# A hybrid decoder block: the input projection as a stage of its own, with its feature-major part in seven half products, and mixers beside another block's output products

## The chip, the cores and the metric

The kernel runs on one core of a Trainium2 chip. The core has a matrix engine (TensorE, PE in the profile; its weight loads are PEld), three engines for element-wise work (VectorE or DVE, ScalarE or ACT, GpSimd or POOL) and a queue for transfers (SyncE or SP). Matrix products write to PSUM, everything else lies in SBUF or in DRAM. The metric is the device time of one execution in microseconds, the median of several runs.

## What is computed

A sequence of 2048 rows of 1024 values passes one decoder block, in float32. The first half is two mixers side by side over one input projection; the second half is a gated feed-forward part, which the change leaves alone.

```python
mod = c @ w_ada + b_ada                      # shift, scale, gate for both halves
h = modulate(rms_norm(x, g_pre_mix), shift_m, scale_m)
proj = h @ w_in                              # 1024 -> 4872 columns
q_a, k_a, v_a, q_m, k_m, v_m, o_m, i_m, f_m, g_a, g_m = jnp.split(proj, ...)
y_a = sliding_window_attention(rope(q_a), rope(k_a), v_a, sinks)      # window 128
q_m, k_m = split(silu(causal_depthwise_conv([q_m, k_m])))             # 4 taps
y_m = sigmoid(o_m) * head_layer_norm(mlstm_chunkwise(q_m, k_m, v_m, i_m, f_m))
merged = sigmoid(g_a) * (y_a @ w_branch_attn) + sigmoid(g_m) * (y_m @ w_branch_mlstm)
x = x + gate_m * rms_norm(merged @ w_out, g_post_mix)
h2 = modulate(rms_norm(x, g_pre_ffn), shift_f, scale_f)
x = x + gate_f * rms_norm((silu(h2 @ w_ffn_gate) * (h2 @ w_ffn_up)) @ w_ffn_down, g_post_ffn)
```

## The kernel before

Each operand of a large product is split into a rounded part and a rest (`hi`, `lo`, type float32r), and a product is three matrix instructions, hi x hi, hi x lo and lo x hi (`mm3`, L273), each of 128 rows of weights and 512 columns. The weights come by DMA in pieces of about 1 MB (`raw`), ScalarE makes `hi` (L259, L256, L1120) and VectorE `lo` (L260, L257, L1121).

The first half goes block by block (`block`, L656), four blocks of 512 rows. In a block come, in this order: q, k and v of the attention and v of the mLSTM with tokens on the partitions ("token-major", `token_group`, L308: 96, 96 and 96 instructions, those of k, v and the gates 264 columns wide); gate A, the mLSTM's q and k, and its output gate with features on the partitions ("feature-major", `feature_tiles`, L302); branch A (`branch_tiles`, L1016); gate B, feature-major again; branch B; and `w_out` with the norm and the residual (`residual_out`, L518). Feature-major are 28 tiles of 128 columns, each 8 slices of k times three instructions. They read the transposed, normed and modulated rows `hhi` and `hlo`, which `hprep` (L477) makes for the next block while `residual_out` runs.

The mixers are written as generators: `q_stream`, `k_stream`, `gates`, `attention` (L797), `chunk_state` (L916), `chunk_out` (L951). `spawn` puts one on a list, and `tick` (L223), called behind every three matrix instructions, takes the next step of each generator that is due by a clock `now`, which adds up estimated instruction times; the number that a generator yields is its distance to the next step (L38 to L43). `finish` (L230) takes all steps that are left at once. So attention is spread over the products of v, gate A and so on, the mLSTM over the branch and gate B products, and the modulation's weights (`ada_stream`, L448) over everything. The order written so is a priority; the framework's scheduler then fixes each engine's order of instructions and may let one that is ready go ahead.

Buffers: nine of 8 KB per partition (`big`), six of 2 KB (`tx`), nine of 2 KB (`tm`), two for raw weights, four for splits; four PSUM banks for products (`acc`) and four for all else (`mix`). Gates, convolution outputs and branch results of a block stay in `big` buffers from their product to their use.

The feed-forward part works on 1024 rows at once and already uses seven half products for eight (the Winograd form of Strassen's scheme): both operands are cut in two along k and along rows or columns, `PROD` (L1098) lists the seven pairs, `a_operands` (L1259) makes the weight sums on VectorE, `h_combine` (L1198) the sums of h, and `combine` (L1319) adds the products to the four quarters of the result. It has its own loop `run2` (L1130), which runs behind that of the first half (`run`, L342).

## Time and profile before

| what | value |
|---|---|
| median of 3 runs | 2773.7 us (2771.84 to 2776.06) |
| the profiled execution, its time | 2771.54 us |
| its span, first to last instruction | 2769.8 us |
| ScalarE busy | 1233.1 us, 45% |
| GpSimd busy | 153.1 us, 6% |
| DMA | 402.63 MB, 145 GB/s over the span |
| transfers of `w_in` | 76 of 1024 KB, 5.1 us to landing |
| mean granted clock of TensorE | 0.994 |

In the rows of the profile a line begins with the line of the program, the engine and the operation; then come output and inputs by the program's names, the shapes, and the count. Behind the bar stand the busy time in us, the mean duration of one in ns, and the idle time of that engine just before these instructions with what ended it. The rows by stretch give, for each engine, busy us and the number of instructions, then TensorE's granted clock, the share of the DMA engines and the GB/s. Records of matrix instructions overlap, since they are pipelined.

### The profile page before, as it was taken

Reading aid. Unit: us, or ns where it says so; the run is one execution under the profiler, and the core shown is the slowest. Engines: PE = TensorE matmul, PEld = TensorE weight load, DVE = VectorE, ACT = ScalarE, POOL = GpSimd, SP = SyncE. Lnnn points to the kernel's source line nnn. Section 1 sums busy time; section 2 is a strip of 40 time slices with the busy share of each in tenths; the row PEclk is TensorE's granted clock in tenths of the full one; section 3 lists DMA queues with packets and bytes.
Section 4 is the critical chain, followed back from the end, with each engine's and each line's share of the span. In section 5 each row is a group of like instructions: output and inputs, shape, how many; then the busy total and the mean of one; then the engine's idle time right before and its main releaser. Section 6 shows DMA issues by size and latency. Waiting matters only on the chain.

```text
span 2769.8 us, 35110 instructions
## 1 busy us (share of the span) xinstructions
PE 2704.9 (98%) x12654; PEld 2199.7 (79%) x12654; DVE 1922.7 (69%) x3802; ACT 1233.1 (45%) x2285; POOL 153.1 (6%) x201
## 2 busy tenths in 40 slices
PE   6999999999999999999999999999999999999998
PEld 4778878788877888768887888887777888888886
DVE  7768657587674876657776777776676767666456
ACT  4543365433554335544363343334554333333444
POOL 2100001001010010110100000000000000000000
PEclk9999999999999999999999999999999999999999
DMA  7233353242552424523356555545666333233566
GB/s 236 88 111 103 100 180 123 80 137 80 169 163 65 135 86 139 180 67 97 98 168 216 172 176 181 175 152 194 203 236 210 130 102 108 98 111 131 189 212 213
DMA packets 280533, 402.63 MB, mean 145 GB/s; under 512 B 19220, under 2 KB 176536, under 8 KB 280360
## 3 DMA queue, kind: packets, MB, share of 16 engines
q1 hardware_dynamic: 280360, 400.40, 44.3%
q8 instruction: 99, 1.62, 0.2%
q14 instruction: 74, 0.61, 0.1%
HBM read 320.62 MB, written 79.73 MB: 145 GB/s over the span
## 4 chain that ended last, share of the span: by engine, by line
PE 87%; DVE 5%; DMA 4%; ACT 2%; issue 1%; POOL 0%; SPq 0%; DVEq 0%; POOLq 0%; ACTq 0%
PE acc L204 63%; PE mix L204 22%; PE mix L209 2%; DVE hl L1121 1%; DMA raw<-in_w_ffn_down_dram 1%; DVE tm L424 1%; DMA tx<-in_w_ada_dram 0%; ACT hl L1120 0%; DMA raw<-in_w_ffn_gate_dram 0%; DMA raw<-in_w_in_dram 0%; DMA raw<-as_d 0%; DMA x1n<-tx 0%; ACT big L1222 0%; POOL rs L472 0%; DMA w<-x 0%
## 5 line engine op out<-in xcount | busy, mean ns | idle before, releaser
L1120 ACT CAST hl<-raw 128x512 fp32r<-128x512 f32 x564 | 337.1, 620 | 400.2 <-PE mix L204 173.3
L1121 DVE TENSOR_TENSOR hl<-raw,hl 128x512 fp32r<-128x512 f32 x564 | 377.1, 687 | 169.5 <-ACT hl L1120 167.0
L259 ACT CAST whi<-raw 128x1024 fp32r<-128x1024 f32 (+1 forms) x208 | 212.1, 1020 | 501.0 <-PE acc L204 439.1
L260 DVE TENSOR_TENSOR wlo<-raw,whi 128x1024 fp32r<-128x1024 f32 (+1 forms) x208 | 247.4, 1189 | 181.0 <-ACT whi L259 178.2
L204 PE MATMUL acc<-hhi,wlo 128*128 128x512 f32 x896 | 353.9, 395 | 0.0
L204 PE MATMUL acc<-hhi,whi 128*128 128x512 f32 x896 | 352.4, 393 | 0.0
L204 PE MATMUL acc<-hlo,whi 128*128 128x512 f32 x896 | 351.8, 393 | 0.0
L204 PE MATMUL acc<-big,hl 128*128 128x512 f32 x1056 | 254.0, 389 | 0.6 <-ACT w L1328 0.6
L204 PE MATMUL acc<-hl,hl 128*128 128x512 f32 x1008 | 237.0, 393 | 6.9 <-DVE hl L1121 4.3
L204 PEld LDWEIGHTS acc<-big,hl 128*128 128x128 f32 x1056 | 198.0, 188 | 42.3 <-ACT w L1328 1.1
L204 PEld LDWEIGHTS acc<-hl,hl 128*128 128x128 f32 x1008 | 187.1, 188 | 52.6 <-DVE hl L1121 9.5
L204 PEld LDWEIGHTS acc<-hhi,wlo 128*128 128x128 f32 x896 | 168.3, 188 | 42.4 <-issue 8.1
L204 PE MATMUL mix<-big,hl 128*128 128x512 f32 x704 | 197.6, 392 | 3.2 <-DVE big L1257 3.2
L204 PEld LDWEIGHTS acc<-hlo,whi 128*128 128x128 f32 x896 | 168.3, 188 | 37.8 <-issue 3.2
L204 PEld LDWEIGHTS acc<-hhi,whi 128*128 128x128 f32 x896 | 168.4, 188 | 37.2 <-issue 4.1
L204 PE MATMUL mix<-hl,hl 128*128 128x512 f32 x792 | 182.4, 390 | 2.0 <-ACT hl L1120 1.3
L204 PEld LDWEIGHTS mix<-hl,hl 128*128 128x128 f32 x792 | 148.0, 188 | 35.5 <-DVE hl L1121 2.7
L204 PE MATMUL acc<-whi,big 128*128 128x512 f32 x512 | 166.0, 396 | 0.0
L204 PE MATMUL acc<-big,whi 128*128 128x512 f32 x512 | 158.4, 394 | 0.0
L204 PEld LDWEIGHTS mix<-big,hl 128*128 128x128 f32 x704 | 132.9, 189 | 32.0 <-DVE big L1257 4.4
L204 PE MATMUL acc<-whi,hhi 128*128 128x512 f32 (+1 forms) x384 | 133.3, 373 | 22.1 <-DVE tx L530 8.9
L204 PE MATMUL acc<-wlo,hhi 128*128 128x512 f32 (+1 forms) x384 | 140.7, 370 | 2.6 <-DVE wlo L260 2.6
(335 smaller groups left out, 4746.6 us busy)
## 6 DMA issues: line engine op xcount, KB each, us to landing
raw<-in_w_in_dram SPq DMA_DIRECT2D x76, 1024.0 KB, 5.1
as_d<-w SPq DMA_DIRECT2D x154, 256.0 KB, 2.2
raw<-as_d SPq DMA_DIRECT2D x70, 512.0 KB, 3.5
raw<-in_w_ffn_gate_dram SPq DMA_DIRECT2D x22, 1024.0 KB, 5.3
raw<-in_w_ffn_up_dram SPq DMA_DIRECT2D x22, 1024.0 KB, 6.3
raw<-ws_d SPq DMA_DIRECT2D x40, 512.0 KB, 4.3
tx<-in_w_ada_dram SPq DMA_DIRECT2D x64, 256.0 KB, 3.1
raw<-in_w_out_dram SPq DMA_DIRECT2D x16, 1024.0 KB, 5.1
```

The costliest lines, as they stand in the source:

```text
L204: T.matmul(o, lhsT=lhsT, rhs=rhs, start=start, stop=stop, skip_group_check=resumed)
L209: T.transpose(o, i, ident[:k, :k])
L259: A.copy(hv, src)
L260: V.tensor_tensor(lv, src, hv.bitcast(F32), op=ALU.subtract)
L424: V.scalar_tensor_tensor(acc, raw[:, k, :], c_, acc, op0=ALU.mult, op1=ALU.add)
L1120: A.copy(v(hi), src)
L1121: V.tensor_tensor(v(lo), src, v(hi).bitcast(F32), op=ALU.subtract)
```

## The change

The input projection becomes a stage in front of the mixers. It goes over two halves of 1024 rows (`feature_major(j)`), and its feature-major columns (28 tiles) are made by `pair_parts`, the seven products of the feed-forward part, two column tiles and two blocks of 512 rows at a time. The sums of h that this needs come from a new generator `ha_stream`; the normed rows of the third and the fourth block go through DRAM (`norm_stream`, `xn_d`). The quarter of h that the half products don't use as it is (first half of the features, second block of the pair) goes to DRAM for the token-major products (`h12_d`), and so does the last quarter of the second pair until its buffer is free (`h22_d`). The token-major columns are made with eight full products as before, block by block (`token_major(b)`), ahead of, between and behind the two feature-major stages. All results of the projection are written to DRAM: `q_d`, `kv_d`, `vm_d`, and `fm_d` for the two gates (the sigmoid is taken first), the convolved q and k, and the output gate. In the convolution the first tap goes to ScalarE; the scale of the output gate goes there too.

The mixers of a block are one generator, `mixers(b)`, which loads what it needs from DRAM: first rotary tables, then k, the gates, q, the attention, and then the mLSTM. `mixers(0)` is spawned in front of `token_major(3)`, and `mixers(b + 1)` at the start of `merge(b)`. `merge(b)` holds the branch products of block b, A and B now by turns, and `w_out` with the residual; its gates are loaded from `fm_d` into `tx` buffers. The generators' distances are as before. The gains of the residual (`gg_m`) and the pools of the mixers are opened behind `token_major(2)`, in the memory of the projection stage. `run2` goes; one loop `run` takes both halves.

The core of the diff:

```diff
...
+    def row_norms(xb):
+
+        ss = small.tile([P, 4], F32, tag="ss", name=nm("ss"), bufs=4)
+        for t in range(2):
+            for hf in range(2):
+                junk = tx([P, 512])
+                A.activation(junk, xb[:, t, hf * 512:(hf + 1) * 512], AF.Square, accum_out=ss[:, 2 * hf + t:2 * hf + t + 1])
+        V.tensor_tensor(ss[:, 0:2], ss[:, 0:2], ss[:, 2:4], op=ALU.add)
+        r = rsqrt_of_sumsq(ss[:, 0:2], 2)
+        for t in range(2):
+            A.activation(xb[:, t, :], xb[:, t, :], AF.Copy, scale=r[:, t:t + 1])
+
...
+    q_d = [tc.dram_tile([TB, 512], F32, name=f"q_d{b}") for b in range(NBLK)]
+    kv_d = [tc.dram_tile([TB, 264], F32, name=f"kv_d{b}") for b in range(NBLK)]
+    vm_d = [tc.dram_tile([TB, 512], F32, name=f"vm_d{b}") for b in range(NBLK)]
+    fm_d = {n: [tc.dram_tile([P, w, TB], F32, name=f"{n}_d{b}") for b in range(NBLK)]
+            for n, w in (("ga", 8), ("gm", 8), ("qk", 8), ("om", 4))}
+    xn_d = {b: tc.dram_tile([TB, D], F32, name=f"xn_d{b}") for b in range(2, NBLK)}
+    h12_d = [tc.dram_tile([P, 2, 4, TB], F32, name=f"h12_d{j}") for j in range(NB2)]
+    h22_d = tc.dram_tile([P, 2, 4, TB], F32, name="h22_d")
+
+    hhi = hpool.tile([P, KD, TB], F32R, tag="hhi", name="hhi")
+    hlo = hpool.tile([P, KD, TB], F32R, tag="hlo", name="hlo")
+    hat = [hap.tile([P, 4, TB], F32R, name=f"ha{x}") for x in ("T2h", "T2l", "T4h")]
+    hap.tile([P, 8], F32, name="hap_end")
+    HA = {"11": [hhi[:, :4, :], hlo[:, :4, :]], "21": [hhi[:, 4:, :], hlo[:, 4:, :]], "T2": hat[:2], "T4": [hat[2], None],
+          "T1": [None, None], "T3": [None, None], "22": [None, None]}
+
...
+        for k in range(4):
+            v = {}
+            for i in range(1 - j if j < 2 else 0, 2):
+                for half in range(2):
+                    kk = k + 4 * half
+                    if j:
+                        xk = unit().rearrange("p (t c) -> p t c", t=NT)
+                        nc.sync.dma_start(xk, xn_d[2 * j + i][:, kk * P:(kk + 1) * P].rearrange("(t p) c -> p t c", p=P))
+                    v[half, i] = xk if j else None
+            if j:
+                yield 3000.0
+            for half, i in v:
+                kk = k + 4 * half
+                ps = mix_tile()
+                for t in range(NT):
+                    transpose(ps[:, t * P:(t + 1) * P], v[half, i][:, t, :] if j else xb[t // 2][:, t % 2, kk * P:(kk + 1) * P])
+                q = unit()
+                A.activation(q, ps, AF.Identity, scale=s1[:, kk:kk + 1], bias=sh1[:, kk:kk + 1])
+                v[half, i] = q
+                yield 1200.0
+
+            def halves(name):
+                return ha_part(name, 0)[:, k, :], ha_part(name, 1)[:, k, :]
+
+            def known(name):
+                return [p_.bitcast(F32) for p_ in halves(name)]
+
+            t1 = unit()
+            if j:
+                for half, name in ((0, "11"), (1, "21")):
+                    split_unit(v[half, 0], *halves(name))
+                    yield 1200.0
+                V.tensor_tensor(t1, v[0, 1], v[0, 0], op=ALU.subtract)
+            else:
+                h_, l_ = known("11")
+                V.tensor_tensor(t1, v[0, 1], h_, op=ALU.subtract)
+                V.tensor_tensor(t1, t1, l_, op=ALU.subtract)
+            t2 = unit()
+            V.tensor_tensor(t2, v[1, 1], t1, op=ALU.subtract)
+            split_unit(t2, *halves("T2"))
+            yield 1200.0
+            t4 = unit()
+            if j:
+                V.tensor_tensor(t4, v[1, 0], t2, op=ALU.subtract)
+            else:
+                h_, l_ = known("21")
+                V.tensor_tensor(t4, h_, t2, op=ALU.subtract)
+                V.tensor_tensor(t4, t4, l_, op=ALU.add)
+            split_unit(t4, *halves("T4"))
+            yield 1200.0
+            split_unit(t1, *halves("T1"))
+            yield 1200.0
+            V.tensor_tensor(t2, v[1, 1], v[0, 1], op=ALU.subtract)
+            split_unit(t2, *halves("T3"))
+            yield 1200.0
+            for name, d_, half in (("22", h22_d if j else None, 1), ("12", h12_d[j], 0)):
+                if d_ is None:
+                    split_unit(v[half, 1], *halves(name))
+                else:
+                    hl = [au([P, TB], F32R) for _ in range(2)]
+                    split_unit(v[half, 1], *hl)
+                    for i in range(2):
+                        nc.sync.dma_start(d_[:, i, k, :], hl[i].bitcast(F32))
+                yield 1200.0
+
...
+    def token_major(b, lhs):
+
+        def stash(dst, n):
+            def evac(t, ps):
+                u = unit()
+                A.copy(u[:, :n], ps[:, :n])
+                nc.sync.dma_start(dst[t * P:(t + 1) * P, :], u[:, :n])
+            return evac
+
...
+    def lhs_second(kk, t):
+        return tuple(p_[:, kk % 4, t * P:(t + 1) * P] for p_ in (F["h12"] if kk < 4 else HA["22"]))
+
+    def load_h12(j):
+        F["h12"] = [big([4, TB], F32R) for _ in range(2)]
+        for i in range(2):
+            nc.sync.dma_start(F["h12"][i].bitcast(F32), h12_d[j][:, i])
+
...
+        for kind, p in (("ga", 0), ("ga", 1), ("qk", 0), ("ga", 2), ("ga", 3), ("qk", 1), ("gm", 0), ("gm", 1), ("qk", 2),
+                        ("gm", 2), ("qk", 3), ("gm", 3), ("om", 0), ("om", 1)):
+            c0 = {"ga": C_GA, "gm": C_GM, "qk": C_QM, "om": C_OM}[kind] + p * 256
...
+                def taps():
+                    V.tensor_copy(u[:, 0:3], hist[:, i, :])
+                    V.tensor_copy(hist[:, i, :], u[:, TB:TB + 3])
+                    ac = st["ac"] = unit()
+                    A.activation(ac, u[:, 0:TB], AF.Identity, scale=col("conv_w", i), bias=col("conv_b", i))
+                    for q in range(1, 4):
+                        V.scalar_tensor_tensor(ac, u[:, q:q + TB], col("conv_w", q * 8 + i), ac, op0=ALU.mult, op1=ALU.add)
+
+                def silu():
+                    sg = unit()
+                    A.activation(sg, st["ac"], AF.Sigmoid)
+                    V.scalar_tensor_tensor(sg, st["ac"], 1.0 if i < 4 else MD ** -0.5, sg, op0=ALU.mult, op1=ALU.mult)
+                    put("qk", b, i, sg)
+
+                later.extend([taps, silu])
...
+            for part in pair_parts(raw_cols(w_in, KD, c0, 256), HA, new, done):
+                part.weave = True
+                part.after = a_step
+                yield part
+
...
+        p0.close()
+        F["mpool"] = p1.enter_context(tc.tile_pool(name="mpool", bufs=1, reuse_waits="tile"))
+        MX["gg"] = F["mpool"].tile([P, D], F32, name="gg_m")
+        F["tpool"] = p1.enter_context(tc.tile_pool(name="tpool", bufs=1, reuse_waits="tile"))
+        kvp = MX["kvp"] = p1k.enter_context(tc.tile_pool(name="kvp", bufs=1, side="right", reuse_waits="tile"))
...
+        def q_all(t):
+            raw = tm([P, HQ * HD])
+            nc.sync.dma_start(raw, q_d[b][t * P:(t + 1) * P, :])
+            yield 3000.0
+            yield from q_stream(t, rope(raw, HQ, t))
...
+        yield from wait([spawn(k_stream(t), 1000.0 * t) for t in range(NT)])
+        gs = spawn(gates(), 2000.0)
+        for t in range(NT):
+            nc.sync.dma_start(vmt[:, t, :, :MD], vm_d[b][t * P:(t + 1) * P, :].rearrange("p (h d) -> p h d", h=MH))
+        yield from wait([spawn(q_all(t), 3000.0 * t) for t in range(NT)])
+        att = [spawn(attention_pair((0, 2)), L_QK), spawn(attention_pair((1, 3)), L_QK + L_ATT2)]
+        for n, kind, i0 in (("km", "qk", 4), ("qm", "qk", 0), ("om", "om", 0)):
+            nc.sync.dma_start(big_of(n), fm_d[kind][b][:, i0:i0 + 4, :])
+        yield from wait(att + [gs])
+        yield from mlstm()
+        yield from wait(R["outs"])
...
+        def begin():
+            finish([R["mx"]])
+            if not last:
+                RB[b + 1]["mx"] = spawn(mixers(b + 1), 500.0)
+                R["mh"], R["ml"] = ([t[:, :4, :], t[:, 4:, :]] for t in
+                                    (hpool.tile([P, KD, TB], F32R, tag=g, name=nm(g)) for g in ("hhi", "hlo")))
+            else:
+                finish(R_ada)
+                R["mh"], R["ml"] = ([big([4, TB], F32R) for _ in range(2)] for _ in range(2))
+                open_hc()
+
+        yield begin
...
+                        gs_ = [tx([P, TB]) for _ in range(2)]
+                        for j in range(2):
+                            nc.sync.dma_start(gs_[j], fm_d[gate][b][:, i + j, :])
...
+        for i, (pa, pm) in enumerate(zip(branch(w_ba, True, ("yah", "yal"), "ga", evac_a), branch(w_bm, False, ("ymh", "yml"), "gm", evac_m))):
+            if last and i == 2:
+                yield lambda: R.update(hc=spawn(h_combine(0, *HC_FROM_MIXER), 3000.0))
+            yield pa
+            yield pm
+        yield from residual_out(KD, lambda kk, t: tuple(R[m][kk // 4][:, kk % 4, t * P:(t + 1) * P] for m in ("mh", "ml")),
+                                a["w_out"][0], big, load_rows(x_d[b * TB:(b + 1) * TB, :], last), MX, x1[b],
+                                None if last else x1n[b], tm if last else tx)
...
+    def program():
+        for ch in ADA:
+            yield lambda ch=ch: first_h(*ch)
+        yield lambda: F.update(ha=spawn(ha_stream(0), 2000.0))
+        yield from token_major(0, lhs_first)
+        yield lambda: finish([F["ha"]])
+
+        def beside_first():
+            F["nx"] = spawn(norm_stream(), 4000.0)
+            R_ada.append(spawn(ada_stream([(2, "gate"), (4, "scale"), (3, "shift"), (5, "gate")], 3300.0), 20000.0))
+
+        yield beside_first
+        for j in range(NB2):
+            yield from feature_major(j)
+            yield lambda j=j: load_h12(j)
+            if j == 0:
+                def next_ha():
+                    finish([F["nx"]])
+                    F["ha"] = spawn(ha_stream(1), 0.0)
+
+                yield next_ha
+                yield from token_major(1, lhs_second)
+                yield lambda: finish([F["ha"]])
+                yield rest_of_ha
+        yield flush_later
+        yield from token_major(2, lhs_first)
+        yield lambda: finish(R_ada)
+        yield open_mixers
+        yield lambda: RB[0].update(mx=spawn(mixers(0), 500.0))
+        yield from token_major(3, lhs_second)
+        for b in range(NBLK):
+            yield from merge(b)
+        yield open_ffn
         yield rest_of_hc
         yield load_gg
         for b2 in range(NB2):
             yield from gate_up(b2)
             yield from down(b2)
 
...
```

457 lines of the change are left out of this document (193 added, 264 removed).

## The prediction

> **What bounds the kernel now.** I read the page first, then the stretches of 50 us one after another, then the waits of TensorE, then the order of time of single engines where the change cuts in.
>
> ```profile
> span 2769.8 us, 35110 instructions
> PE 2704.9 (98%) x12654; PEld 2199.7 (79%) x12654; DVE 1922.7 (69%) x3802; ACT 1233.1 (45%) x2285; POOL 153.1 (6%) x201
> PE 87%; DVE 5%; DMA 4%; ACT 2%; issue 1%; POOL 0%; SPq 0%; DVEq 0%; POOLq 0%; ACTq 0%
> L204 PE MATMUL acc<-hhi,wlo 128*128 128x512 f32 x896 | 353.9, 395 | 0.0
> ```
>
> TensorE is busy 98% of the span and carries 87% of the chain that ended last. The busy time of a group can't be used as its price, since a product is recorded with 395 ns while others overlap it. The price is the spacing: products in a stretch that holds nothing else.
>
> ```profile
> core 0: us, PE busy (x) PEld busy (x) DVE busy (x) ACT busy (x) POOL busy (x), PEclk, DMA share, GB/s
> 400.00:450.00 50.00, 46.01 (x262) 39.31 (x261) 33.58 (x98) 28.23 (x60) 4.89 (x9) 0.97 0.66 212
> 750.00:800.00 50.00, 44.99 (x249) 38.45 (x248) 36.14 (x106) 29.92 (x64) 6.02 (x12) 1.00 0.76 248
> 900.00:950.00 50.00, 50.00 (x222) 41.41 (x221) 39.49 (x69) 18.38 (x27) 0.00 (x0) 1.00 0.46 132
> 1100.00:1150.00 50.00, 46.74 (x250) 39.98 (x248) 32.69 (x81) 26.18 (x54) 4.52 (x8) 0.97 0.72 240
> 1450.00:1500.00 50.00, 44.24 (x179) 34.81 (x178) 35.23 (x62) 18.76 (x35) 3.19 (x4) 0.93 0.66 237
> 2200.00:2250.00 50.00, 50.00 (x222) 41.42 (x221) 33.41 (x54) 17.57 (x31) 0.00 (x0) 1.00 0.27 90
> ```
>
> Both the feature-major stretch (900 to 950) and the FFN stretch, which already uses seven products for eight (2200 to 2250), hold 222 products in 50 us: **0.2252 us each**, clock 1.00. So a product of 512 columns costs the same in either scheme. TensorE loses time only at the seams between blocks: 4.0, 5.0 and 3.3 us idle where a block begins (400, 750, 1100) and 5.8 us where the FFN begins (1450). The granted clock of 0.97, 0.97 and 0.93 in three of these stretches costs 1.5, 1.5 and 3.5 us more. That makes 24.6 us. The largest of the waits behind it:
>
> ```profile
> PE acc L204 <- DVE tx L530: 8.9, 6, 2.3
> PE acc L204 <- ACT w L1322: 2.0, 1, 2.0
> ```
>
> **The change, part by part.** *Products removed.* Groups hhi,wlo, hhi,whi and hlo,whi are the feature-major part: 28 tiles of 128 columns, 8 slices of k, 4 blocks, 896 in each of three groups, 2688 together. Seven for eight leaves 2352. 336 fewer at 0.2252 us are **75.7 us**, all on the engine that sets the end. Transposes stay 128 in number for h.
>
> *Work added beside those products.* One pair of column tiles for 1024 rows is 84 products, 18.9 us. VectorE gets for it 7 splits, 4 sums of weights and 4 sums of products, each an operation of 128x512.
>
> ```profile
> L1121 DVE TENSOR_TENSOR hl<-raw,hl 128x512 fp32r<-128x512 f32 x564 | 377.1, 687 | 169.5 <-ACT hl L1120 167.0
> L1257 DVE TENSOR_TENSOR big<-w,big 128x512 fp32r<-128x512 f32 x8 | 5.2, 686 | 7.0 <-DMA w<-hc_d 7.0
> 1487.86 2.49 DVE L1257 TENSOR_TENSOR big<-w,big 128x512 fp32r<-128x512 f32 x4
> L899 DVE SCALAR_TENSOR_TENSOR tx<-tx,cols,tx 128x512 f32<-128x512 f32 x96 | 72.0, 750 | 2.7
> L424 DVE SCALAR_TENSOR_TENSOR acc_ada<-tx,c_sb,acc_ada 128x256 f32<-128x256 f32 x112 | 56.6, 506 | 7.7 <-DMA tx<-in_w_ada_dram 6.5
> ```
>
> Four such operations in a row took 2.49 us: (2.49 - 0.686) / 3 = 0.60 us from start to start, though each is recorded with 0.686. So a pair costs VectorE 15 x 0.60 = 9.0 us of 18.9, 126 us over 14 pairs (265 us). The convolution for 1024 rows adds three of the L899 kind and one more sum per tile, 16 tiles, 16 x (3 x 0.67 + 0.60 + 0.2) = 45 us, and the modulation (L424, 112 of them, nearly all beside the first of the two stages) up to 47 us: at most 218 of 265 us, hidden. ScalarE has less than half of its time taken in the like FFN stretch (17.6 of 50 us) and gains a few operations of 0.6 us per pair. Stalls here: 0 to 10 us by bursts; I take 2.
>
> *Operands of the half products.* ha_stream makes T1 to T4 of h: 12 operations of VectorE per k, 4 k, 48 x 0.60 = 29 us, once beside token_major(0) and once beside token_major(1), each of 192 products of 512 and 96 of 264 columns: 192 x 0.2252 + 96 x 0.116 (by columns) = 54.3 us. VectorE has 11 us of weight splits of its own there, so it fits; but the stream starts behind an x load, and the first products need its results at once. Cover gone, it would be up to 10 us at each; the load of h12 (2 MB) in front of token_major(1) another 10 us at the 212 GB/s of the 400 to 450 stretch. Behind that first product of token_major(1) the 191 others of its group stand in TensorE's order, and their evacuation. Bounds 0 and 30; I take 10, since the inputs are in DRAM long before and the order is drawn ahead, as this shows:
>
> ```profile
> 612.26 0.28 DVE L570 TENSOR_TENSOR tx<-inv_freq,pos 128x128 f32<-128x128 f32 x1
> L1066 DVE TENSOR_TENSOR big<-acc,big x8: 683/692/692, 685.6 to 704.2; 128x512 f32<-128x512 f32 x8
> ```
>
> The rotary tables (L570) stand in the program behind all of L1066, yet they ran 73 us before it: ready work is pulled forward on an engine that has room.
>
> *Traffic.* What was kept in SBUF now goes through DRAM: gates, convolution outputs, q, kv, vm, the normed x, h12 and h22, by count of bytes some 97 MB, against 29 MB of weight reads saved. 68 MB on 402 MB. The busiest stretch above moved 248 GB/s; a merge with its mixer needs about 24 MB in 139 us, 173 GB/s. SP issues about 340 transfers more; two in a row took it 0.87 us:
>
> ```profile
> 1472.74 0.87 SPq L543 DMA_DIRECT2D x<-tx  x2
> ```
>
> That is 150 us of SP over the kernel, and with the old ones some 76 issues or 33 us in a merge. Price nothing as long as a store that waits for VectorE doesn't hold the gate loads (`gs_`) behind it; the sum products need those within 2.7 us. The scratch pool `tx` of six is shared by gates (up to six wanted), rotary tables (four) and output rows, and that is what is late next at each seam: it is in the 10 us per merge below.
>
> *Mixers moved.* Before, a mixer lay beside the whole block. Now mixers(0) lies beside token_major(3), mixers(b+1) beside merge(b). This is where the saving can be lost. What is the mixer worth? One block took from here to here:
>
> ```profile
> 65.33 0.39 PE L204 MATMUL acc<-whi,hhi 128*128 128x264 f32 x1 [0.30 <-ACT tm L675]
> 421.89 0.28 PE L204 MATMUL acc<-whi,hhi 128*128 128x264 f32 x1
> 777.63 0.28 PE L204 MATMUL acc<-whi,hhi 128*128 128x264 f32 x1
> 1136.01 0.28 PE L204 MATMUL acc<-whi,hhi 128*128 128x264 f32 x1
> 32.87 1.07 PE L209 MATMUL mix<-ident,big 128*128 128x128 f32 x8
> L260 DVE TENSOR_TENSOR wlo<-raw,whi 128x1024 fp32r<-128x1024 f32 x192 | 236.1, 1230 | 178.2 <-ACT whi L259 175.4 <-PE mix L204 1.4 <-PE acc L204 0.2
> L507 DVE TENSOR_TENSOR hlo<-tx,hhi 128x512 fp32r<-128x512 f32 x24 | 16.6, 691 | 13.1 <-ACT tx L506 12.8
> 437.00:787.00 350.00, 344.99 (x1695) 278.86 (x1695) 241.87 (x554) 165.74 (x313) 33.38 (x34) 1.00 0.38 121
> ```
>
> (1136.01 - 65.33) / 3 = 356.9 us a block. Of it 672 + 192 + 384 = 1248 products are 281.0, kv 11.1, 32 transposes at 1.07 / 8 us 4.3, the seam about 6: the mixer's own TensorE work is the rest, less some modulation, **52 us**. So merge(b) with mixers(b+1) is 384 x 0.2252 + 52 = **138.5 us** of TensorE, and token_major(3) with mixers(0) 54.3 + 52 = **106 us**.
>
> VectorE over a block is 241.87 x 356.9 / 350 = 246.6 us. What does not go into the merge is taken off: 28 feature splits of 1.23 us (34), the splits of q, kv and v by their widths (13), a quarter of the convolution (18 of L899, 10 for its other operations by width), h's splits (16.6 / 3, 6) and a quarter of the modulation (14). **151 us** stay for the merge and its mixer. Run back to back they would take 151 x 0.60 / 0.686 = 132 us. So beside 138.5 us of TensorE stand 132 to 151 us of VectorE: the stage goes from one bound to two nearly equal ones.
>
> The Trainium skill, "VectorE: DVE Perf Modes", section "The DRAIN you can't avoid", says that the next operation does not start until the pipe of the former is empty, which speaks against the lower figure. By that rule VectorE would need the 151 us or more and the second rival below would follow. The trace has 0.60 us from start to start where 0.686 is recorded, so I side with 132 where the queue is full.
>
> Length counts beside work. In the second block attention and the mLSTM ran like this, first product or transpose to last write:
>
> ```profile
> 448.37 0.38 PE L204 MATMUL mix<-kth,big 64*128 64x256 f32 x1
> 527.90 0.59 ACT L863 CAST big<-mix 128x512 fp32r<-128x512 f32 x1 [2.67 <-PE mix L204]
> 593.26 0.27 PE L209 MATMUL mix<-ident,big 128*128 128x128 f32 x1
> 675.99 0.69 DVE L999 TENSOR_TENSOR big<-tm,big 128x512 fp32r<-128x512 f32 x1
> ```
>
> Attention 80.1 us, mLSTM 83.4 us, and from kv's first product (421.89) to attention 26.5 us: 190 us end to end with nothing pressing, against 138.5 and 106 us. The first product of branch m waits for the last of it; behind that product the rest of the merge stands in TensorE's order, except the branch a products ordered in front, and w_out waits for them. For a merge the bound below is 0, the bound above 190 - 26.5 (drawn into the former window) - 138.5 = 25 us; I take 10, nearer to 0 because attention and mLSTM don't depend on each other and the next mixer starts while the last one ends. For mixers(0) the bounds are 0 and 190 - 106 - 11 (four tiles of branch a at 12 products) = 73 us; I take 25, as its loads and tables can begin in token_major(2), where VectorE has 40 us free.
>
> *Sum* against the profiled execution: 2769.8 - 75.7 - 24.6 (old seams) + 2 + 10 + 25 + 3 x 10 + 9 (merge(3) to FFN, as the old seam there) = 2745.5; 1.7 us lie around the span (profiled run 2771.5), and the median of the runs is 2.2 above that run, so **2749 us**.
>
> **The rivals.** *1. The saving arrives almost whole*: stalls stay at the old 25 us; for it speaks that TensorE never idled beside the same mixers away from the seams (50.00 of 50 in 900 to 950); against it, that half the cover is gone. 2769.8 - 75.7 + 3.9 = **2698**. *2. VectorE sets the pace of the merges*: 151 us at 95% use are 159, 20.5 over TensorE, three times, and 10 for mixers(0) in addition: stalls 2 + 10 + 35 + 61.5 + 9 = 117.5, and 2769.8 - 100.3 + 117.5 + 3.9 = **2791**. For it speaks the sum of 151; against it the spacing of 0.60. *3. Slower, by the length of the mixer's chain*: it stays serial at its old pace, TensorE finishes merge(b) and waits at the first branch m product of merge(b+1). 73 + 3 x 25 + 21 elsewhere = 169: 2769.8 - 100.3 + 169 + 3.9 = **2842**. It decides from the point where all new stalls pass 100 us. Against it: the part of the chain that is waiting for its turn shrinks when TensorE is free. *4. The products don't become fewer or run slower per product*: the FFN rows at the same 222 per 50 us speak against it; 0.02.
>
> **How the numbers follow.** Forecast 0.44, rival 1 0.17, rival 2 0.15, rival 3 0.22, rival 4 0.02. The forecast's own range is 2710 to 2785. For 8 in 10 I go from 2692 (rival 1 inside) to 2835 (rival 2 inside, the upper half of rival 3 outside). A measurement of this kernel tells about 0.2% (5.5 us) from no change. Faster: 0.44 x 0.92 + 0.17 = 0.58; same 0.04; the rest slower, 0.38.
>
> **What would show it.** Right: 2352 products in the two feature stages, each stage near 265 us at 222 per 50 us; TensorE gaps gathered behind token_major(2) and at each branch m. Rival 1: no gaps there. Rival 2: VectorE above 95% in the merges with TensorE waiting for splits (the wlo and hl groups). Rival 3: VectorE well below 90% while TensorE waits for L999's and L864's successors or for the cast in front of them. The prediction is wrong if the feature stages themselves stall by more than 20 us each, or if the first wait behind token_major(2) exceeds 73 us.

## The result and the profile after

The changed kernel takes 2949.5 us (median of 4 runs, 2948.61 to 2954.91) against 2773.62 us: a ratio of 1.0638, 95% interval 1.0619 to 1.0656. It is 176 us slower, and 114 us above the upper end of the predicted range. In the texts below "after" is this kernel.

The page of after: span, busy time of the engines, and the chain that ended last by engine.

```profile
span 2946.8 us, 35780 instructions
PE 2709.5 (92%) x12318; PEld 2191.8 (74%) x12318; DVE 2046.2 (69%) x4130; ACT 1275.1 (43%) x2475; POOL 157.5 (5%) x205
PE 48%; DVE 8%; DMA 6%; ACT 3%; issue 2%; POOL 1%; SPq 0%; POOLq 0%; DVEq 0%; ACTq 0%
```

TensorE has exactly 336 matrix instructions fewer (12654 - 12318), yet its busy time did not fall: 2709.5 us after 2704.9. Its idle time went from 64.9 us (2769.8 - 2704.9) to 237.3. So the 177.0 us between the spans are 172.4 us of idle time and 4.6 us of busy time; and since the missing products are worth 75.7 us, the others took 80.3 us longer. Most of that is the granted clock, 0.960 in the mean after 0.994: busy time x (1 - clock), added up over stretches of 20 us, is 78 us in after and 11 in before. The chain that ended last runs through TensorE for 48% and no longer 87%.

The stretches of after, by stage: one clean piece of the second feature stage, then all projections, token_major(3) with mixers(0), merge(0) to merge(2), merge(3), the FFN. Columns: sum, busy us of each engine, granted clock, share and rate of the DMAs.

```profile
550.00:600.00 50.00, 50.00 (x222) 41.45 (x221) 36.67 (x65) 24.85 (x43) 0.00 (x0) 1.00 0.36 126
...
30.00:810.00 780.00, 744.79 (x3409) 616.56 (x3410) 531.64 (x980) 395.79 (x693) 19.34 (x18) 0.98 0.51 170
810.00:960.00 150.00, 120.22 (x601) 95.38 (x599) 103.72 (x350) 52.99 (x140) 21.61 (x21) 0.83 0.38 119
960.00:1150.00 190.00, 162.12 (x796) 122.56 (x796) 144.52 (x395) 72.96 (x179) 29.94 (x32) 0.95 0.42 132
1150.00:1350.00 200.00, 155.34 (x732) 118.79 (x732) 143.98 (x401) 73.00 (x181) 30.65 (x32) 0.86 0.42 131
1350.00:1553.00 203.00, 154.72 (x761) 119.34 (x762) 145.41 (x395) 80.50 (x193) 29.66 (x32) 0.87 0.42 135
1553.00:1660.00 107.00, 96.42 (x427) 78.35 (x426) 77.53 (x122) 49.09 (x82) 3.64 (x5) 0.98 0.66 222
1660.00:2947.00 1287.00, 1263.87 (x5556) 1035.09 (x5554) 884.44 (x1449) 534.91 (x979) 14.87 (x20) 1.00 0.50 167
```

The feature stage is what was forecast, 222 products in 50 us. 161.2 of the 237.3 us of idle time lie between 810 and 1660 us, in the five stages with a mixer or a merge, and so does most of the low clock. A merge beside a mixer takes some 200 us where TensorE has 138.5 us of work. VectorE is busy 144 of 200 us there, 72%: less than TensorE, and far from full on the average.

What TensorE waited for in these stages (us in total, times, longest), and the times of three VectorE lines: L584 opens a mixer (its rotary tables), L1171 is the mixer's last write (yml), L544 takes the output rows out of PSUM.

```profile
PE mix L222 <- POOL tm L1058: 26.3, 15, 5.1
PE acc L217 <- DVE tx L1253: 19.9, 3, 9.7
PE mix L217 <- DVE tm L1162: 19.0, 8, 3.2
PE acc L217 <- DVE sx L526: 15.2, 2, 10.7
```

```profile
L584 DVE TENSOR_TENSOR tx<-inv_freq,pos x2: 284/284/285, 1153.3 to 1354.3; 128x128 f32<-128x128 f32 x2
...
L1171 DVE TENSOR_TENSOR big<-tm,big x4: 681/688/693, 1299.4 to 1331.1; 128x512 fp32r<-128x512 f32 x4
...
L544 DVE TENSOR_TENSOR big<-acc,gg_m x4: 677/678/682, 1300.0 to 1302.4; 128x512 f32<-128x512 f32 x4
```

Two of the four waits are steps inside the mixer (L1058 of attention, L1162 of the mLSTM); L1253 and L526 are the seam. Merge(1) starts with the tables at 1153.3 us and merge(2) at 1354.3: a pitch of 201.0 us. Within it the mixer runs from 1153.3 to 1331.8, 178 us. And the first half of the output rows leaves PSUM at 1300, right behind the first write to yml, though the squares of the same four tiles were taken at 1226.8 to 1234.4:

```profile
1226.76 0.61 ACT L542 ACTIVATE tx<-acc 128x512 f32<-128x512 f32 x1
...
1233.83 0.60 ACT L542 ACTIVATE tx<-acc 128x512 f32<-128x512 f32 x1
...
1299.38 0.68 DVE L1171 TENSOR_TENSOR big<-tm,big 128x512 fp32r<-128x512 f32 x1
1299.98 1.28 DVE L544 TENSOR_TENSOR big<-acc,gg_m 128x512 f32<-128x512 f32 x2
```

For 65 us all four accumulation banks are full, so no product of the merge can run; TensorE has only the mixer.

A third thing shows at the seam, in the order of time of the DMA queue and of VectorE:

```profile
1169.51 1.82 SPq L1238 DMA_DIRECT2D tx<-gm_d  x2
...
1169.52 0.23 DVE L592 TENSOR_SCALAR tx<-tx 128x128 f32<-128x128 f32 x1
1172.11 0.69 DVE L1253 TENSOR_TENSOR tx<-acc,tx 128x512 f32<-128x512 f32 x1 [0.87 <-DMA tx<-gm_d]
```

The gates of the first mLSTM branch tile are asked for at 1169.5, when the rotary tables (L582 to L628), which hold four of the six small buffers, let go of one; TensorE stands 9.7 us for the evacuation behind it.

### The profile page after: what moved, and what is told of

Its sections match the earlier page's. It is cut to its first block, busy times and chain, and to the rows that moved or that the text cites. A ratio compares the mean times of both kernels' runs of the same rounds, so it can differ in the third digit from the quotient of the medians.

```text
span 2946.8 us, 35780 instructions
## 1 busy us (share of the span) xinstructions
PE 2709.5 (92%) x12318; PEld 2191.8 (74%) x12318; DVE 2046.2 (69%) x4130; ACT 1275.1 (43%) x2475; POOL 157.5 (5%) x205
## 4 chain that ended last, share of the span: by engine, by line
PE 48%; DVE 8%; DMA 6%; ACT 3%; issue 2%; POOL 1%; SPq 0%; POOLq 0%; DVEq 0%; ACTq 0%
PE acc L217 30%; PE mix L217 17%; DVE hl L1295 1%; PE mix L222 1%; ACT tm L1054 1%; DMA raw<-in_w_ffn_down_dram 1%; DMA w<-x 1%; DVE wlo L273 1%; ACT hl L1294 1%; DMA raw<-ws_d 1%; DMA tm<-negm_d 0%; DMA ws_d<-big 0%; DMA tx<-in_x_dram 0%; DMA hc_d<-tm 0%; DMA x1n<-tx 0%
## 5 line engine op out<-in xcount | busy, mean ns | idle before, releaser
L217 PE MATMUL acc<-big,hl 128*128 128x512 f32 x1728 | 416.2, 390 | 2.5 <-ACT w L1451 2.0
L217 PEld LDWEIGHTS acc<-big,hl 128*128 128x128 f32 x1728 | 324.1, 188 | 72.0 <-ACT w L1451 3.8
L217 PE MATMUL mix<-big,hl 128*128 128x512 f32 x1152 | 322.6, 392 | 5.1 <-DVE big L1383 5.1
L272 ACT CAST whi<-raw 128x1024 fp32r<-128x1024 f32 (+1 forms) x96 | 94.0, 980 | 183.6 <-PE acc L217 169.1
L217 PE MATMUL acc<-whi,big 128*128 128x512 f32 (+1 forms) x512 | 152.2, 378 | 4.2 <-ACT tm L775 4.2
L273 DVE TENSOR_TENSOR wlo<-raw,whi 128x1024 fp32r<-128x1024 f32 (+1 forms) x96 | 108.8, 1133 | 67.2 <-ACT whi L272 66.8
L217 PE MATMUL acc<-whi,hlo 128*128 128x512 f32 (+1 forms) x384 | 143.0, 379 | 3.8 <-POOL hlo L521 3.8
L217 PE MATMUL mix<-hc,hl 128*128 128x512 f32 x528 | 134.3, 390 | 1.3 <-DVE hl L1295 0.7
L217 PE MATMUL acc<-hc,hl 128*128 128x512 f32 x528 | 127.0, 389 | 0.0
L217 PE MATMUL acc<-hcT2h,hl 128*128 128x512 f32 x352 | 116.2, 391 | 2.9 <-ACT w L1445 2.9
```

Of the source, the lines that this page charges most:

```text
L217: T.matmul(o, lhsT=lhsT, rhs=rhs, start=start, stop=stop, skip_group_check=resumed)
L272: A.copy(hv, src)
L273: V.tensor_tensor(lv, src, hv.bitcast(F32), op=ALU.subtract)
```

## The experiments

Three theories. **Chain**: a mixer is one chain of dependent steps, four of them in a row set the time from 810 to 1553 us. **Buffers and order**: the merges are long because of what was just shown (blocked banks, tables in the small buffers). **Load**: an engine's work sets the pace. Times are medians of 4 runs unless a range of another number is given, the ratio, with its 95% interval, is to the kernel before in the same session.

**1. One buffer for the tables.**

```
-        y, t1, t2, fr = t_(), t_(), t_(), t_()          # four tx tiles
+        scr = tx([P, 4 * NT * 32]).rearrange("p (s t f) -> p s t f", s=4, t=NT)
+        y, t1, t2, fr = (scr[:, i] for i in range(4))
```

> The four scratch tiles of the rope tables become quarters of one, so that they hold one of the six small buffers and not four. Buffer theory: the gate rows of the next branch product wait for these four (the load of gm is issued only when the tables' step at L592 lets go of its tile, 1169.5 us), and with them TensorE: 21.0 us idle in 1125 to 1175 and 24.1 us in 1325 to 1375, and the clock falls to 0.70 and 0.66 there. Two seams shrink by 15 to 20 us each: 2910 to 2920 us. Chain theory (the mixers' own length sets the pitch of the merges): the tables end no sooner, 2940 to 2955 us.

2927.5 us, ratio 1.0561 (1.0545 to 1.0577): 22 us gained, 11 in the mean at each of two seams. The small buffers were short, at less than the expected 15 to 20 us a seam. Edit 1 is in all runs below except the first of experiment 2 and experiment 4.

**2. The output rows' buffer reserved early.** In merge, ahead of the output products; runs without and with edit 1:

```
+        if not last:
+            yield lambda: R.update(keep=big([NT, 512]))
```

> The buffer that takes the first half of the output rows is reserved when the branch products are through, ahead of the two that take the mLSTM's output of the next block. Buffer theory: in the changed kernel the squares of the first half are taken at 1227 to 1235 us, and the products leave their four banks only at 1300, right behind the first write to yml; with the reservation they leave at about 1240, the second half follows, and each merge gives back 15 to 35 us of idle time and low clock: 2850 to 2905 us. Chain theory: the second half comes 40 to 60 us sooner, but the next merge still starts when the mixers end, so the hole only moves behind the second half: 2935 to 2955 us.

> The two edits together. Buffer theory: the gains add, 2810 to 2880 us. Chain theory: 2925 to 2950 us, and TensorE idles in one piece between the second half of one merge and the first branch product of the next.

2953.2 us (1.0632 to 1.0668) alone and 2927.2 us (1.0546 to 1.0577) with edit 1: nothing. But the edit did not do what it was meant to do: L544 still ran right behind the first write to yml (1290 us in the second run). So these two runs decide nothing about the blocked banks.

**3. All attention branch tiles ahead of the mLSTM ones**, with edits 1 and 2; the attention part waits in mh and ml instead of in a small buffer:

```
             yield pa
-            yield pm
+            second.append(pm)        # merges 0 to 2
+        yield from second
```

> Both edits, and in merges 0 to 2 all eight attention branch products stand ahead of the eight mLSTM ones; the attention part waits in the high and low buffers of the sum (16 more splits: 8 x (0.65 us ScalarE + 0.60 us VectorE) a merge, and 8 more additions). The buffers of the block before that the attention's output takes over come free some 25 us sooner (after 96 products and not 192), and fewer small buffers are held. Buffer theory: 10 to 20 us a merge better than both edits alone, 2770 to 2850 us. Chain theory: the attention of the next block ends some 20 us sooner, and so does the merge after it: also some 15 us a merge better than both edits alone. If neither, VectorE's added work shows and the time is 0 to 15 us above that of both edits.

2959.9 us, ratio 1.0677 (1.0658 to 1.0696): 33 us worse than edits 1 and 2. That is near the time of the 48 VectorE operations that this order adds: VectorE is busy 2069.7 us, 29 more than with edits 1 and 2. Whatever the next mixer gained by getting its buffers earlier did not pay for them.

**4. Nothing beside the mixer.** Mixers(b + 1) starts behind merge(b), all else as in after:

```
-                RB[b + 1]["mx"] = spawn(mixers(b + 1), 500.0)                      # in begin
+            yield lambda: RB[b + 1].update(mx=spawn(mixers(b + 1), 0.0))           # last step of merge
```

> The mixer of block b+1 starts when the merge of block b is through, so nothing lies beside it. Chain theory (a mixer is one chain of dependent steps, some 170 to 180 us from the rotary tables to the last write of yml, and the four of them in a row set 810 to 1553 us): alone it is little shorter, 150 to 180 us, and each merge adds its 86.5 us: three times (150 to 180 + 95 - 200) more than the changed kernel, 3085 to 3175 us. Contention theory (the mixer is long only because it shares the engines with the output products): alone it takes 100 to 120 us, and the time is 2935 to 2995 us.

3062.0 us (two runs, 3060.1 to 3064.0; ratio 1.1044, 1.1022 to 1.1066). Mixers and merges one by one, in stretches of this run, with the mixer's first and last VectorE line:

```profile
1071.00:1202.00 131.00, 72.92 (x373) 51.06 (x374) 97.29 (x320) 41.65 (x124) 23.78 (x25) 0.68 0.28 87
1202.00:1302.00 100.00, 84.53 (x360) 69.07 (x360) 49.85 (x81) 33.63 (x57) 3.70 (x7) 0.91 0.44 147
...
L584 DVE TENSOR_TENSOR tx<-inv_freq,pos x1: 284/284/284, 1070.6 to 1070.6; 128x128 f32<-128x128 f32 x1
...
L1171 DVE TENSOR_TENSOR big<-tm,big x4: 674/686/693, 1188.2 to 1201.7; 128x512 fp32r<-128x512 f32 x4
```

A mixer alone is 131 us long, a merge alone 100 us. That lies between the two theories: the mixer really is a chain (TensorE and VectorE both wait in it), but beside a merge it grows by 47 us. Woven, the two take 201 us instead of 231: the overlap hides only 30. And of its 131 us the chain spends 97.3 in VectorE, while the merge has 49.9 of VectorE's time.

**5. The mLSTM behind the first of the two attention streams**, with edit 1:

```
-        yield from wait(att + [gs])
+        yield from wait(att[:1] + [gs])
         yield from mlstm()
+        yield from wait(att)
```

> With the one-tile tables; the mLSTM starts when the first of the two attention streams is through, and no longer behind both. Chain theory: the chain gets shorter by what the second stream runs past the first, 5 to 15 us a mixer, and every mixer counts: 2870 to 2907 us. If the merges' own engines set the pace: 2920 to 2935 us, as with the tables alone.

2896.0 us, ratio 1.0443 (1.0425 to 1.0460): 31.5 us below edit 1, as the chain theory says. But the edit does two things. In merge(1) the mixer is 5 us shorter, 167 us from the tables to the last write after 172 with edit 1. And since the mLSTM's first write comes sooner, the first half of the output rows leaves its banks sooner too: 66 us behind the squares, and no longer 78. So the chain's length and the blocked banks both have a part in this gain.

**6. The evacuation by ScalarE**, with edits 1 and 2; then without edit 2 but with the next block's tables ahead of the mLSTM (the last two lines):

```
+            if hf == 0 and gg is MX:
+                A.copy(y, ps)
+                G.tensor_tensor(y, y, gg["gg"][:, :512], op=ALU.mult)
+                return
...
+        if b + 1 < NBLK:
+            tables[b + 1] = rope_tables(b + 1)
```

> With the one-tile tables and the early reservation; the first half of the output rows leaves its banks by ScalarE and is multiplied by GpSimd, so that it does not stand in VectorE's order behind the mLSTM's first output. The four banks come free right behind the squares (about 1212 us where the two edits together had 1290), and the second half's 96 products can run beside attention and mLSTM. Chain theory: the start of the mixer's chain is not touched, but the 20 to 25 us between its last write and the next merge's first branch product shrink by 10 to 20 us: 2865 to 2900 us. VectorE-order theory (the late evacuation is what makes the merges long): 40 to 60 us a merge, 2750 to 2810 us. No effect: 2920 to 2935 us.

> As the run before without the early reservation; and the rotary tables of the next block (40 small VectorE operations, 8 to 18 us on the chip) are made ahead of this block's mLSTM and no longer at the head of the next mixer. Chain theory: the tables only change places in the chain, -5 to +5 us against the ScalarE evacuation alone. If the tables' wait for a small buffer at the seam is what counts, 10 us less a merge, 2835 to 2870 us.

2921.2 us (1.0520 to 1.0552) and 2903.1 us (1.0456 to 1.0487). The first is what was expected of no effect. Its order on ScalarE gives the reason, and that of edit 2:

```profile
1204.06 0.59 ACT L542 ACTIVATE tx<-acc 128x512 f32<-128x512 f32 x1
...
1280.65 0.62 ACT L1172 CAST big<-tm 128x512 fp32r<-128x512 f32 x1 [6.16 <-DVE tm L1171]
1281.18 2.04 ACT L545 COPY big<-acc 128x512 f32<-128x512 f32 x4
```

Another engine, and again the copies stand right behind the first write to the mLSTM's output (L1172, into ymh); between them and the squares ScalarE was mostly idle. What the two have in common is the kind of buffer, big. If such buffers are handed out in the order of the first writes and not of the reservations, the reserved one gets its place only behind ymh and yml; experiment 7 tries this. In the second run the tables' move gained 18 us, more than the chain theory had (-5 to +5 us) and less than the other side (2835 to 2870 us).

**7. The reserved buffer written at once**, with edit 1:

```
+        def reserve():
+            R["keep"] = big([NT, 512])
+            G.memset(R["keep"][:, 0, 0:1], 0.0)
```

> With the one-tile tables; the buffer of the first half of the output rows is reserved early as before and at once written by GpSimd in one column, since the built order of the former runs suggests that buffers of this kind are handed out in the order of their first write. If that is so, the first half now leaves its banks some 60 us sooner and the second half's 96 products run beside attention and mLSTM, as intended before. Chain theory: only the 20 to 25 us between the mixer's last write and the next merge's first evacuation can shrink, 5 to 15 us a merge, 2880 to 2915 us. VectorE-order theory (the four blocked banks make the merges long): 40 us a merge, 2790 to 2820 us.

2902.8 us, ratio 1.0471 (1.0456 to 1.0487): 25 us below edit 1, as the chain theory has it, and some 80 us above the upper end of the other theory. So the order of the first writes decides. Now the banks come free early and the merges start 178.2 us apart:

```profile
L582 DVE TENSOR_TENSOR tx<-inv_freq,pos x2: 279/281/283, 1113.6 to 1291.8; 128x128 f32<-128x128 f32 x2
...
L544 DVE TENSOR_TENSOR big<-acc,gg_m x4: 685/692/692, 1220.6 to 1229.7; 128x512 f32<-128x512 f32 x4
...
L1169 DVE TENSOR_TENSOR big<-tm,big x4: 684/693/693, 1302.6 to 1324.9; 128x512 fp32r<-128x512 f32 x4
```

But the mixer that opens at 1113.6 ends at 1325.6 (L1169 is here what L1171 was): 212 us, longer than before. What the second half's products gained, the mixer lost in part.

**8. Products away.** The third product of each branch term left out in merges 0 to 2, with edit 1, and with edits 1 and 7:

```
-        mm(ps, l[1], r[0], False, last)
+        if n == 3:                                   # 2 for the branches, 3 elsewhere
+            mm(ps, l[1], r[0], False, last)
```

> With the one-tile tables; leaves out the third product of each branch term (low weights by high input) in merges 0 to 2, 64 of 192 products each: 192 x 0.2252 = 43.2 us of TensorE less, everything else stays. If TensorE's load set the pace of the merges: 2927.5 - 43 = 2884 us. Chain theory: the mixers don't get shorter, 2912 to 2930 us.

> The early written buffer and the run with 43.2 us fewer products together, since the products left out had also brought the first half's evacuation forward (1213 us), which the early written buffer does by itself (2902.8 us). Leaves out the third product of each branch term in merges 0 to 2. If TensorE's load counts in full: 2860 us. Chain theory: 2885 to 2903 us, since the mixer sets the pace once the banks are free; the earlier run's 2889.7 would then have been mostly the banks.

2889.7 us (1.0411 to 1.0442) and 2886.9 us (1.0385 to 1.0416). The first looks like load, 38 of 43.2 us; but its banks also came free at 1213 us, which the edit did not aim at. At equal buffers, against edit 7, the same 43.2 us of TensorE are worth 16 (19 by the ratios, since the kernel before took 3.6 us longer in the later session). TensorE alone does not set the pace.

**9. Edits together**: 1, 7 and the earlier mLSTM; then the tables ahead of the mLSTM too.

> The one-tile tables, the early written buffer, and the mLSTM that starts behind the first attention stream. Chain theory: the two gains concern different stretches (the chain, and what follows it) and add: 2850 to 2885 us. If the second half took room that the shorter chain needs: 2885 to 2900 us, no better than the earlier mLSTM alone (2896).

> As the run before, and the rotary tables of the next block are made between the attention and the mLSTM of this one. With the ScalarE evacuation the tables' move was worth 18 us; chain theory: the head of each chain loses the tables, while VectorE has room beside the mLSTM: 10 to 20 us below the run before, 2835 to 2870 us. Still above the kernel before, because three chains of some 160 us take the place of 138.5 us of TensorE work.

2889.5 us (1.0407 to 1.0441) and 2890.0 us (1.0411 to 1.0442), hardly below the earlier mLSTM alone. The gains of 25, 31.5 and 18 us do not add: the repairs give back the same time for the most part. For experiments 5 and 7 a part of it is the blocked banks, which both free; with the banks free already the earlier mLSTM is worth 13 us (2902.8 to 2889.5).

**10. More products for the hole at the mixer's end**: the order of experiment 3 with edits 1 and 7, and with all of them.

> The one-tile tables, the early written buffer, and all attention branch products of merges 0 to 2 ahead of the mLSTM ones (as in the run before that had it without the early written buffer). Hole theory: at the end of each mixer TensorE has only two tiles of the next merge to work on (two evacuations at 1291 to 1297 us, the next at 1332), since tiles of the two branches alternate and the mLSTM ones wait for yml; of 1280 to 1320 us it was busy 21 of 40, at a clock of 0.53 and 0.59. With eight tiles instead of two, 72 more products of 0.2252 us can fill the hole: up to 16 us a merge, 2850 to 2890 us. Chain theory: what fills the hole is not missing elsewhere, the mixer is as long as before, 2895 to 2910 us.

> All edits: one-tile tables, early written buffer, attention branch first, mLSTM behind the first attention stream, tables of the next block ahead of the mLSTM. Hole theory: 10 to 16 us a merge below the same without the attention branch first (2890): 2840 to 2865 us. Chain theory: 2880 to 2895 us.

2906.6 us (1.0460 to 1.0495) and 2903.9 us (1.0455 to 1.0489), the second 14 us above the same without this order and outside both ranges. All eight tiles now ran ahead of the mixer's last write, and nothing was gained: the mixers ended some 10 us later (1335.8 us for 1325.6 in merge(1)). The first of the two runs, the stretch where they ran and the one at the next mixer's end, and that mixer's last write:

```profile
1120.00:1140.00 20.00, 11.73 (x64) 10.39 (x62) 20.00 (x55) 7.52 (x12) 4.07 (x2) 0.82 0.50 162
...
1300.00:1320.00 20.00, 10.30 (x54) 9.04 (x52) 19.00 (x60) 6.98 (x10) 4.00 (x3) 0.83 0.48 157
...
L1169 DVE TENSOR_TENSOR big<-tm,big x4: 676/692/693, 1310.6 to 1335.1; 128x512 fp32r<-128x512 f32 x4
```

VectorE, 72% busy on the average, is full or nearly so here: 20.00 and 19.00 of 20 us, while TensorE is busy half the time. But this order adds 48 VectorE operations, 30 us of VectorE's time over the three merges (2071.9 us after 2042.3); in experiment 7 the same two windows hold 17.69 and 18.11 us. So the runs don't tell whether the hole was worth nothing or whether its gain went into these operations.

**11. VectorE work away**: as 8 with edits 1 and 7, and the low halves of the branch weights, which nothing uses any more, are not made:

```
-                    yield Piece(raw, (lambda t, i2=i2: t[:, :, i2 * P:(i2 + 2) * P]), [4, 256], mms)
+                    yield Part(raw, high, mms)       # high: the cast alone
```

> As the run with fewer products at equal buffers (2886.9), and the low halves of the branch weights aren't made either in merges 0 to 2: 24 VectorE operations of 1.25 us fewer, 30 us of VectorE in all; leaves out the third product of each branch term and its weights. If VectorE's other work stands in front of the mixer's steps and so counts more than TensorE's products (16 us gained for 43.2): 20 to 30 us gained, 2857 to 2867 us. If VectorE's load does not matter: 2880 to 2890 us.

2859.7 us, ratio 1.0310 (1.0293 to 1.0327): 27 us gained (25 by the ratios) by 24 operations of 1.25 us, 30 us. VectorE's work beside the mixer counts eight to nine tenths, TensorE's about four (16 to 19 of 43.2 us). The products no longer wait for these halves either, but between 810 and 1620 us the run before shows no wait of TensorE for them. The pieces also take one split buffer now and not two; what that is worth was not tried.

**12. A longer mixer by work on GpSimd.** With edits 1 and 7, in attention:

```
+                for _ in range(3):
+                    G.tensor_tensor(sc[g], sc[g], ones.unsqueeze(1).to_broadcast([P, GQ, P]), op=ALU.mult)
```

> The one-tile tables and the early written buffer (2902.8), and in attention the GpSimd step between the exponentials and the transpositions is followed by three multiplications by one, 1.07 us each: 8 x 3 x 1.07 = 25.7 us of GpSimd a mixer on an engine that is busy 5% of the span; no other engine gets work. Chain theory: every mixer becomes 13 to 26 us longer and all four count, 2955 to 3005 us. If the engines' load sets the pace: 2900 to 2915 us.

2939.3 us, ratio 1.0599 (1.0583 to 1.0614): 36.5 us, 9.1 a mixer. No theory's number, but the chain's sign. The added operations took 1.44 us each and not 1.07:

```profile
L1058 POOL TENSOR_TENSOR tm<-tm,ones 128x512 f32<-128x512 f32 x96 | 136.4, 1444 | 1.2
```

136.4 us of GpSimd, 34.1 a mixer, of which a good quarter reached the end. But the expectation that no other engine gets work did not hold. VectorE ran the same 4130 operations as in experiment 7 and was busy 2076.6 us after 2042.3, 34 us more; among them are the low halves of the weights:

```profile
L273 DVE TENSOR_TENSOR wlo<-raw,whi 128x1024 fp32r<-128x1024 f32 x80 | 99.3, 1241 | 43.3 <-ACT whi L272 37.8 <-ACT tm L1037 2.7 <-PE mix L222 2.6
...
L273 DVE TENSOR_TENSOR wlo<-raw,whi 128x1024 fp32r<-128x1024 f32 x80 | 108.6, 1358 | 42.8 <-ACT whi L272 40.1 <-PE mix L222 2.6
```

The first line is experiment 7, the second this run. GpSimd's own step in attention took 1286 ns in the mean after 1105, so the operations of both engines got longer beside each other. At the rate of experiment 11 the 34 us of VectorE alone would account for most of the 36.5. So this run does not show what a longer chain costs by itself.

**13. VectorE work moved to GpSimd**, in the second version of 9: the low halves of the output weights.

```
-            V.tensor_tensor(lv, src, hv.bitcast(F32), op=ALU.subtract)
+            low.tensor_tensor(lv, src, hv.bitcast(F32), op=ALU.subtract)      # low: G for the output weights
```

> All edits that helped (one-tile tables, early written buffer, mLSTM behind the first attention stream, tables of the next block ahead of the mLSTM: 2890 us), and the low halves of the output weights are made by GpSimd in the merges, 8 x 1.25 us of VectorE fewer a merge, at some 4 us each on GpSimd. If VectorE's other work holds up the mixer: 10 to 25 us better, 2865 to 2880 us. If GpSimd's longer operations now stand in front of the attention's own GpSimd step: 2890 to 2920 us.

2895.1 us, ratio 1.0439 (1.0424 to 1.0455): no gain, 5 us above the run that it starts from, and the intervals overlap. 32 operations worth 39 us left VectorE, yet its busy time fell only from 2043.6 to 2037.5 us: the operations that stayed took 33 us longer, as in experiment 12. So VectorE was not relieved, and whether GpSimd's part in the chain also cost time can't be told. No version tried beats the kernel before.

## Why the prediction was wrong, step by step

*Right.* The products: 336 fewer, 0.2252 us each in either scheme, 75.7 us of work gone. The merge's VectorE time: 151 us reckoned, 144 measured. The end of merge(3): 10.6 us idle for 9. That the small buffers would be "late next at each seam": 22 us by experiment 1, though it was lost in a 10 us term. The 0.60 us from start to start also holds in the merges: two L544 in 1.28 us, with 0.68 recorded for each. The Trainium skill, "VectorE: DVE Perf Modes", section "The DRAIN you can't avoid", has the next operation wait until the pipe is empty, and adds that one that is not held starts earlier. The prediction left this addition out; the trace fits it, since the next operation starts some 0.08 us before the recorded end of the former.

*Too small.* Idle time from 30 to 810 us is 35.2 us, where feature stages and operands together had 12. mixers(0) was to stall 25 us, bounds 0 and 73; it was 29.8 us idle, and with a clock of 0.83 on 120.2 busy us another 20. And every stall was priced as waiting alone; the 80.3 us of slower products had no term.

*The step that failed* is "For a merge the bound below is 0, the bound above 190 - 26.5 (drawn into the former window) - 138.5 = 25 us; I take 10". It sets the mixer's length against the stage's TensorE work and lets the longer of the two win. The runs showed that the two add for the most part. Alone 131 and 100 us (experiment 4), woven 201. With the mixer's length alone, 131 us against 138.5, the step would even have given no stall at all. Idle in the three merges: 27.9, 44.7 and 48.3 us, with the clock (busy time x (1 - clock)) 8, 22 and 20 more: 171 us for the 30 of the sum. These 141 us are most of the 201 by which the sum was off (2946.8 for 2745.5).

Why do they add? What the runs support is an account by VectorE: the mixer's 131 us are a chain that is itself in VectorE for 97 of them, and each of the merge's VectorE operations that is placed between two steps of it pushes the rest back. 131 + 50 = 181 us, against 178.2 measured in experiment 7. In after, merge(1) has two parts:

```profile
1180.00:1220.00 40.00, 40.00 (x198) 32.57 (x197) 39.26 (x85) 17.29 (x27) 0.43 (x1) 1.00 0.65 226
1220.00:1300.00 80.00, 59.24 (x295) 40.95 (x293) 52.58 (x158) 30.91 (x107) 19.59 (x18) 0.79 0.18 49
```

For the first 40 us both streams run, TensorE is never idle and VectorE is full, 39.26 us; there, by this account, the mixer is held back. For most of the next 80 us the merge stands at its full banks, the mixer is left alone, and VectorE is busy only 66%. The account also fits that 48 more VectorE operations cost 33 us in experiment 3 (only 4 in experiment 10, where more products ran beside them), and that 30 us less of VectorE gave 27. The other 20 us of the pitch of 201 are where the tables' buffers and the blocked banks were (experiments 1 and 7, 47 us over the kernel). It is an account that fits, not one that was isolated: TensorE's products also count for four tenths, and the two runs with more work on GpSimd (12 and 13) slowed VectorE too and so decide nothing.

*The rivals.* Rival 3 had the place right (VectorE well below 90%, waits at the first branch m product, L1253, 9.7 us) and the sign, at 2842. It counted as length what the mixer was seen to take with room on both sides, and still drew 26.5 us of it into the former merge; with nothing drawn in, four chains of 190 us against 521.5 us of TensorE (106 + 3 x 138.5) would have been 238 us of stalls. Rival 2 was told by "VectorE above 95%", which the averages refute, but it named the right engine: by the account above the wait is for a turn on VectorE and for the result of the turn before. My argument against rival 3, that waiting for a turn shrinks when TensorE is free, looked at the wrong queue. And the row that I quoted for rival 1, 50.00 of 50 us beside the same mixers, showed a mixer spread over 357 us of products, not over 138.5.

## What to carry to other kernels

When dependent work is moved to stand beside less cover, don't compare its length with the cover's busy time: split the chain by engine, and add to its length alone whatever the cover needs of the engine that the chain itself mostly uses; this one case fits it (181 us for 178.2). An average of 72% hides that the engine is full while both streams run and has room only where the chain is left alone. And work that is moved from VectorE to GpSimd is not off VectorE's time until the trace says so: in experiment 13 operations worth 39 us went, and VectorE's busy time fell by 6. And before pricing an overlap, ask whose buffers stand between the two streams: here four of six small buffers and one large one, handed out in the order of first use, cost some 47 us, and could be seen in the order of time as a transfer or a copy that starts on the very microsecond in which another step lets go.

## What was not expected of the hardware

Waiting costs TensorE twice. After 172.4 us more idle time its remaining products took 80.3 us longer, about half a microsecond for each idle one; the other runs with as many products have 0.34 (experiment 4) to 0.56 by the same sum. Short waits can be enough. In after, from 835 to 880, there are two waits of 4 us and then two short ones:

```profile
PE acc L217 <- ACT tm L775: 4.2, 1, 4.2
PE mix L222 <- DVE gt L970: 4.0, 1, 4.0
PE mix L222 <- DVE cl L1005: 1.4, 1, 1.4
PE mix L217 <- DVE big L934: 0.5, 1, 0.5
```

```profile
845.00:850.00 5.00, 5.00 (x26) 0.58 0.43 161
850.00:855.00 5.00, 3.59 (x33) 1.00 0.59 164
855.00:860.00 5.00, 4.54 (x23) 0.61 1.00 421
860.00:865.00 5.00, 5.00 (x21) 0.50 0.95 360
865.00:870.00 5.00, 5.00 (x27) 0.50 0.37 111
870.00:875.00 5.00, 5.00 (x31) 0.69 0.00 0
875.00:880.00 5.00, 5.00 (x30) 1.00 0.32 108
```

Behind the waits of 4 us the products of kv, without a pause from 845, brought the clock back by 850. Between 850 and 856 stand only the waits of 1.4 and 0.5 us, and the clock fell again; then it stayed low through a stretch that shows no idle time at all.

The Trainium skill, "TensorE: Matmul & The Clock Gate", section "What's actually happening", gives a window of about 3.4 us of sustained work after which the full clock is back. The first return agrees with it; the second came after more than 10 us of recorded work. The products in this stretch are those of attention (64 rows) and of kv (264 columns). The kind of product alone is hardly the reason: from 1245, mostly with attention's products of 64 rows, the clock was back at 1.00 within 5 us.

```profile
1245.00:1250.00 5.00, 5.00 (x31) 0.64 0.00 0
1250.00:1255.00 5.00, 3.96 (x24) 1.00 0.05 13
```

What kept it low stays open; since ends of products are modelled in the profile, short gaps may be hidden.
